# A decoder layer's second norm: rows scaled on ScalarE, the norm's weights put on in the copy of turned rows, and each block turned once

## The chip, the cores and the metric

One core of a Trainium2 chip runs the whole kernel. The metric is the device time of one execution in microseconds (us), lower is better. Five engines work side by side, each in the order of its own queue: TensorE (PE, with its weight loads PEld), VectorE (DVE), ScalarE (ACT), GpSimd (POOL) and SyncE (SP), which issues most transfers. Matmuls write to PSUM; the other tiles lie in SBUF.

## The reference, cut to what matters

One layer on 512 rows of 1024 numbers. What the change touches lies between the attention half and the MLP:

```python
def _rms_norm(x, gain):
    y = xf * lax.rsqrt(jnp.mean(xf * xf, axis=-1, keepdims=True) + NORM_EPS)
    return y * gain
# after the output projection o:
x1 = x + _rms_norm(o, attn_post_norm)
h  = _rms_norm(x1, ffn_pre_norm)          # "the second norm"
a, u = h @ ffn_w_gate, h @ ffn_w_up       # both 1024 x 4096
# then conv over three rows on a, gelu(a) * u, @ ffn_w_down, post norm, residual add
```

So each row of `h` is a row of `x1` times one scalar of that row (1/rms), times a vector of 1024 weights that is the same for all rows.

## The kernel before, in words

All matmuls are done in three passes: every operand is split into a high part (`hi`, a ScalarE copy to the matmul type) and a low part (`lo`, the VectorE difference of the operand and its high part), and hi·hi, hi·lo and lo·hi are added up.

The gate and up products use a scheme with seven products in place of eight (Strassen's kind). The rows of `h` are cut in two halves of 256 rows (half 0 is tiles t = 0, 1; half 1 is t = 2, 3) and in two halves of 512 columns (n = 0, 1). This gives four blocks 11, 21, 12, 22 (first digit the column half, second digit the row half). The right operands of the products are, turned so that columns lie on the partitions: 21, 11, t3, t1, t2, t4, 22, where with p the scaled rows t1 = p12 − p11, t3 = p22 − p12, t2 = p22 − p11 and t4 = p21 − t2. `first_products` does 21 and 11 for two pairs of weight tiles (four products of 24 matmuls), `other_products` the five others. The weights come as `pair` tiles (two transfers of 1 MB, gate and up) in a pool of five 1 MB buffers with tag `v`; `Weights.operand` splits them, hi on ScalarE (L191), lo on VectorE (L194), and GpSimd makes sums and differences of weight blocks (L177). There are four buffers for split weights, given back when a product is done.

The stage of the change: `out_rest` finishes the output projection of a tile (L405 to L407, added on VectorE at L1217). `second_norm(t)` then squares on ScalarE (L1225), takes 1/rms on GpSimd (L1231, after a small VectorE sum at L1228 or L1230), multiplies by the first norm's weights (L1241, GpSimd for t = 1 to 3), adds the residual (L1244, VectorE), squares again, takes the second 1/rms, and writes the normalised rows over `part[t][n]` in one VectorE instruction that multiplies by the scalar and by the weights of the second norm (L1247). The weights lie as rows copied to all partitions in `gains`, one `v` buffer that holds both norms' weights; two transfers of 0.5 MB fill it. `right_operand` turns two tiles of one block with eight 128x128 transposes on TensorE into two PSUM banks (L1257), copies hi from PSUM (L1259) and takes lo from PSUM and hi (L1260). It is called seven times, so there are 56 transposes. `other_operands` takes the differences between scaled rows first (L1284: six on VectorE, two on GpSimd) and turns the results.

A scheduler orders each engine's queue by priorities and by its own estimate of times; `second_norm` and `other_operands` have raised priority. `gpar`, a small tile with a norm's weights by partition, already holds the second norm's weights in its columns 8 to 15; before the change they are not read. Most tiles of 128x512 that are named here come from one pool, `F`, with 18 buffers.

Of the kernel before, what the change touches and what calls it, by code (L numbers as in the profile page):

```python
# [11 lines left out]
F32 = mybir.dt.float32  # L12
BF16 = mybir.dt.bfloat16
F32R = mybir.dt.float32r
AF = mybir.ActivationFunctionType
ALU = mybir.AluOpType
# [3 lines left out]
D = 1024  # L20
# [9 lines left out]
def f32(ap):  # L30
    return ap.bitcast(F32)
# [22 lines left out]
GV = (0,)  # L54
PLO = (1,)
MLO = 1
TS = (3,)
RAWS = 2
WARM = (18, 14, 8)
OWN = (2, 3)  # L60
# [170 lines left out]
def kernel(  # L231
# [6 lines left out]
    vec, act, pool, pe, sp = nc.vector, nc.scalar, nc.gpsimd, nc.tensor, nc.sync  # L238
# [5 lines left out]
    vpool = ctx.enter_context(tc.tile_pool(name="big", bufs=BIGS))  # L244
# [7 lines left out]
    def nm(s):  # L252
        cnt[0] += 1
        return f"{s}_{cnt[0]}"
# [3 lines left out]
    def bank(tag):  # L258
        if tag == "pv":
            turn[0] ^= 1  # L260
            tag = ("va", "vb")[turn[0]]
        return psum.tile([128, 512], F32, tag=tag, name=nm(tag), bufs=1 if tag[0] == "v" else 2)

    def tt(name, tag="F"):
        return acts.tile([128, S], F32R, tag=tag, name=nm(name), bufs={"F": FB, "M": MB, "H": HB}[tag])

    def tf(name):
        return f32(tt(name))
# [14 lines left out]
    def later(*fs):  # L283
        side.extend(fs)
        asked[0] += len(fs)
# [84 lines left out]
    ident = cst.tile([128, 128], F32, name="ident")  # L370
# [33 lines left out]
    def mm3(o, lh, ll, rh, rl, first, last):  # L404
        pe.matmul(o, lh, rh, start=first, stop=False)  # L405
        pe.matmul(o, lh, rl, start=False, stop=False)  # L406
        pe.matmul(o, ll, rh, start=False, stop=last)  # L407

    gpar = cst.tile([128, 16], F32, name="gpar")
# [5 lines left out]
    for n in range(2):  # L415
        ps = bank("sc")
        for _ in range(WARM[n]):
            keep(pe.transpose(ps[:, 0:128], ident, ident))
        if n == 0:
            ps = bank("tr")  # L420
# [35 lines left out]
    def mm_bank():  # L456
        flush(marks.popleft())
        return bank("mm")

    def mm_done():  # L460
        marks.append(asked[0])
# [133 lines left out]
    ps = bank("tr")  # L595
# [41 lines left out]
    part = [[None, None] for _ in range(4)]  # L637
# [225 lines left out]
    gains = []  # L863

    def fill_out():
        for n, a in enumerate((attn_post, ffn_pre)):
            if n == 0:
                gains.append(vpool.tile([128, 2, D], F32, tag="v", name="gains"))
            sp.dma_start(gains[0][:, n, :], a.partition_broadcast(128).rearrange("p a d -> p (a d)"))
        W.open_pairs(vpool)  # L870
        W.spare = {u: lambda: [tt("wa", "H") for _ in range(2)] for u in W.spare}
        for n in range(2):
            ws = [W.take() for _ in range(2)]
            for t in range(4):
                ps = mm_bank()
                sl = slice(128 * t, 128 * t + 128)
                for k in range(4):
                    w = ws[k // 2]
                    mm3(ps, mixT[0][k][:, sl], mixT[1][k][:, sl], w[0][:, k % 2, :], w[1][:, k % 2, :], k == 0, k == 3)
                    if t == 3 and k % 2:  # L880
                        W.free()
                    yield 1
                part[t][n] = tf("part")
                later(lambda ps=ps, t=t, n=n: act.activation(part[t][n], ps, AF.Copy))
                mm_done()
        yield "out"

    def everything():
        yield from fill_moba()
        yield from fill_nsa()  # L890
        yield from fill_diff()
        yield from fill_swa()
        yield from fill_out()
# [69 lines left out]
    class Task:  # L963
        first, mid, second, end, srcs, pv = (), None, (), None, None, None
# [222 lines left out]
    for time, _, f, rate in events:  # L1187
        owed += (time - at) * (cur if at < now else late_rate)
        at = time
        k = int(owed)  # L1190
# [11 lines left out]
    x1 = [fp.tile([128, D], F32, name=f"x1_{t}") for t in range(4)]  # L1202
    for t in range(4):
        act.dma_start(x1[t], x[0, 128 * t:128 * t + 128, :])
    t2pool = ctx.enter_context(tc.tile_pool(name="t2", bufs=XB))
    gpost, gpre = gains[0][:, 0, :], gains[0][:, 1, :]

    flush()
    ws = [W.take() for _ in range(4)]
# [24 lines left out]
    def half_of(a, n):  # L1234
        return a[:, 512 * n:512 * n + 512]

    def second_norm(t):
        r = rstd2(*part[t])
        for n in range(2):
            eng = vec if t in GV else pool  # L1240
            eng.tensor_tensor(part[t][n], part[t][n], half_of(gpost, n), op=ALU.mult)  # L1241
        for n in range(2):
            xh = half_of(x1[t], n)
            vec.scalar_tensor_tensor(xh, part[t][n], r, xh, ALU.mult, ALU.add)  # L1244
        r = rstd2(x1[t])
        for n in range(2):
            vec.scalar_tensor_tensor(part[t][n], half_of(x1[t], n), r, half_of(gpre, n), ALU.mult, ALU.mult)  # L1247

    def right_operand(src, tags, tag):

        hi, lo = [], []
        for m in range(2):
            ps = bank(tags[m])
            for k in range(2):
                for u in range(2):
                    c = 128 * (2 * m + k)
                    pe.transpose(ps[:, 256 * k + 128 * u:256 * k + 128 * u + 128], src[u][:, c:c + 128], ident)  # L1257
            h, l = (t2pool.tile([128, S], F32R, tag="X", name=nm("fT")) if tag == "X" else tt("fT", tag) for _ in range(2))
            act.activation(h, ps, AF.Copy)  # L1259
            vec.tensor_sub(l, ps, f32(h))  # L1260
            for k in range(2):
                hi.append(h[:, 256 * k:256 * k + 256])
                lo.append(l[:, 256 * k:256 * k + 256])
        return hi, lo

    R = {}
    for half in range(2):
        for n in range(2):
            for t in (2 * half, 2 * half + 1):
                out_rest(t, n)  # L1270
            if half:
                W.free(2)
        for t in (2 * half, 2 * half + 1):
            with tc.high_priority(HN):
                second_norm(t)
        if not half:
            R["11"] = right_operand([part[0][0], part[1][0]], ("tr", "pv"), "M")
            R["21"] = right_operand([part[0][1], part[1][1]], ("tr", "pv"), "M")

    def other_operands():  # L1280
        tags = ("tr", "pv")
        p = part
        def less(n, o, a, b):
            (pool if n in TS else vec).tensor_tensor(o, a, b, op=ALU.subtract)  # L1284

        t2 = [tf("t2") for _ in range(2)]
        for t in range(2):
            less(0, p[t][0], p[t + 2][0], p[t][0])
            less(1, p[t + 2][0], p[t + 2][1], p[t + 2][0])
            less(2, t2[t], p[t + 2][1], p[t][0])  # L1290
            less(3, p[t][1], p[t][1], t2[t])
        R["t3"] = right_operand([p[2][0], p[3][0]], tags, "H")
        R["t1"] = right_operand([p[0][0], p[1][0]], tags, "H")
        R["t2"] = right_operand(t2, tags, "H")
        R["t4"] = right_operand([p[0][1], p[1][1]], tags, "H")
        R["22"] = right_operand([p[2][1], p[3][1]], tags, "X")


    acc = []
# [94 lines left out]
    with tc.high_priority(HN):  # L1394
        other_operands()
# [83 lines left out]
```

## Time and profile before

| what | value |
|---|---|
| time, median of 3 runs | 822.89 us (821.38 to 822.95) |
| the profiled execution | 821.32 us, its span 819.5 us |
| instructions | 13505 |
| busy: PE, DVE, ACT, POOL | 781.0, 665.6, 446.9, 338.5 us |

The span is the time from the first to the last instruction in the trace; 1.8 us lie around it. Times within the trace are counted from the span's start. A busy PE is not PE at its peak, and idle time of an engine that nobody waits for costs nothing. The second norm lies between about 270 and 326 us.

### The profile page before, as it was taken

To read this page: it belongs to the slowest core of one execution; us is meant where nothing else is said; L and a number is where in the kernel's file an instruction comes from. 1 tells how busy PE (TensorE), PEld (TensorE's weight loads), DVE (VectorE), ACT (ScalarE), POOL (GpSimd) and SP (SyncE) were. 2 spreads that over 40 slices of the span, in tenths; PEclk is the share of its full clock that TensorE was granted. 3 is DMA by queue.
4 is the path that set the end of the run, shared out by engine and by line. 5 is a ranking of instruction groups with operands and counts; after the bars stand their busy time and mean duration, and the time that the engine had idled before them with its cause. 6 is when DMAs were issued, how large, how long until landed. Compare 5 with 4: busy or idle time off the path is not lost.

```text
span 819.5 us, 13505 instructions
## 1 busy us (share of the span) xinstructions
PE 781.0 (95%) x5087; PEld 712.1 (87%) x5087; DVE 665.6 (81%) x1131; ACT 446.9 (55%) x931; POOL 338.5 (41%) x309
## 2 busy tenths in 40 slices
PE   8999998999989769999999999999999999999995
PEld 8998986997868658988998998998998998998984
DVE  5657768877586999896797797897897987989857
ACT  6657666777676545645554453454454454445532
POOL 5245333336244757343343441461561561563103
PEclk9999999999989979999999999999999999999998
DMA  7455201416211403412114305216116026033212
GB/s 213 121 149 138 64 22 46 129 52 216 80 52 52 154 7 109 145 61 94 52 50 157 103 10 197 67 38 206 43 61 206 18 86 205 1 104 104 69 60 102
DMA packets 72920, 78.76 MB, mean 96 GB/s; under 512 B 7782, under 2 KB 58136, under 8 KB 72856
## 3 DMA queue, kind: packets, MB, share of 16 engines
q1 hardware_dynamic: 71032, 73.71, 29.3%
q10 hardware_dynamic: 1824, 4.20, 1.5%
q8 instruction: 40, 0.66, 0.3%
q14 instruction: 24, 0.20, 0.1%
HBM read 73.71 MB, written 2.10 MB: 93 GB/s over the span
## 4 chain that ended last, share of the span: by engine, by line
PE 57%; DVE 33%; issue 3%; DMA 3%; ACT 2%; POOL 1%; ACTq 0%; DVEq 0%; POOLq 0%
DVE wu L194 13%; PE mm L405 5%; PE mm L406 5%; PE mm L407 4%; DVE y L1362 3%; PE mm L1312 3%; PE mm L1314 3%; PE mm L1313 3%; PE tr L406 3%; PE tr L407 2%; PE sc L1314 2%; PE sc L1313 2%; PE sc L1312 2%; PE tr L405 2%; PE tr L973 2%
## 5 line engine op out<-in xcount | busy, mean ns | idle before, releaser
L194 DVE TENSOR_TENSOR wu<-pair,wu 128x512 fp32r<-128x512 f32 x188 | 174.6, 964 | 15.8 <-ACT wu L191 15.6
L191 ACT ACTIVATE wu<-pair 128x512 fp32r<-128x512 f32 x188 | 108.6, 622 | 76.3 <-PE sc L1314 19.8
L1314 PE MATMUL mm<-fT,wu 128*128 128x256 f32 x488 | 138.3, 283 | 0.7 <-DVE wu L194 0.7
L1312 PE MATMUL mm<-fT,wu 128*128 128x256 f32 x488 | 138.2, 283 | 0.7 <-ACT mo L1343 0.7
L1313 PE MATMUL mm<-fT,wu 128*128 128x256 f32 x488 | 138.2, 283 | 0.0
L1314 PE MATMUL sc<-fT,wu 128*128 128x256 f32 x392 | 111.3, 284 | 0.0
L1313 PE MATMUL sc<-fT,wu 128*128 128x256 f32 x392 | 111.1, 284 | 0.0
L1312 PE MATMUL sc<-fT,wu 128*128 128x256 f32 x392 | 111.0, 284 | 0.0
L152 ACT ACTIVATE wu<-raw 128x512 fp32r<-128x512 f32 (+2 forms) x126 | 71.3, 609 | 67.9 <-DMA raw<-in_ffn_w_down_dram 43.8
L177 POOL TENSOR_TENSOR sum<-pair 128x512 f32<-128x512 f32 x32 | 48.7, 1526 | 141.2 <-DMA pair<-in_ffn_w_up_dram 71.4
L177 POOL TENSOR_TENSOR pair<-sum,pair 128x512 f32<-128x512 f32 x32 | 56.2, 1771 | 116.6 <-DVE wu L194 114.7
L177 POOL TENSOR_TENSOR pair<-pair 128x512 f32<-128x512 f32 x64 | 103.4, 1628 | 2.0
L157 DVE TENSOR_TENSOR wu<-raw,wu 128x512 fp32r<-128x512 f32 (+2 forms) x96 | 73.5, 783 | 35.3 <-ACT wu L152 34.8
L1312 PEld LDWEIGHTS mm<-fT,wu 128*128 128x128 f32 x488 | 93.6, 192 | 1.2 <-ACT mo L1343 0.9
L1314 PEld LDWEIGHTS mm<-fT,wu 128*128 128x128 f32 x488 | 93.6, 192 | 0.9 <-DVE wu L194 0.9
L1313 PEld LDWEIGHTS mm<-fT,wu 128*128 128x128 f32 x488 | 93.6, 192 | 0.3
L941 POOL TENSOR_SCALAR P<-P,rc 128x128 f32<-128x128 f32 (+2 forms) x80 | 42.3, 547 | 84.3 <-DVE rc L1039 39.6
L1313 PEld LDWEIGHTS sc<-fT,wu 128*128 128x128 f32 x392 | 75.2, 192 | 0.3
L1312 PEld LDWEIGHTS sc<-fT,wu 128*128 128x128 f32 x392 | 75.2, 192 | 0.3
L1314 PEld LDWEIGHTS sc<-fT,wu 128*128 128x128 f32 x392 | 75.3, 192 | 0.0
L949 ACT ACTIVATE P<-P,mn 128x128 f32<-128x128 f32 (+2 forms) x96 | 52.1, 543 | 33.2 <-DVE mn L948 32.8
L157 POOL TENSOR_TENSOR wu<-raw,wu 128x512 fp32r<-128x512 f32 (+2 forms) x30 | 40.6, 1356 | 48.4 <-ACT wu L152 44.7
(318 smaller groups left out, 1955.8 us busy)
## 6 DMA issues: line engine op xcount, KB each, us to landing
pair<-in_ffn_w_gate_dram SPq DMA_DIRECT2D x16, 1024.0 KB, 7.7
pair<-in_ffn_w_up_dram SPq DMA_DIRECT2D x16, 1024.0 KB, 5.4
raw<-in_ffn_w_down_dram SPq DMA_DIRECT2D x32, 512.0 KB, 4.1
raw<-in_w_in_dram SPq DMA_DIRECT2D x14, 512.0 KB, 3.9
raw<-in_w_out_dram SPq DMA_DIRECT2D x8, 512.0 KB, 5.4
raw<-in_w_in_dram SPq DMA_DIRECT2D x10, 256.0 KB, 3.2
x<-in_x_dram SPq DMA_DIRECT2D x4, 512.0 KB, 4.6
x<-in_x_dram ACTq DMA_DIRECT2D x4, 512.0 KB
```

Of the source, the lines that this page charges most:

```text
L152: keep(self.nc.scalar.activation(box["h"][:, sl], box["r"][:, sl], AF.Copy))
L157: keep(eng.tensor_tensor(box["l"][:, sl], box["r"][:, sl], f32(box["h"][:, sl]), op=ALU.subtract))
L177: self.nc.gpsimd.tensor_tensor(block(g, out), block(g, a), block(g, b), op=op)
L191: self.nc.scalar.activation(box["h"][g], block(g, src), AF.Copy)
L194: self.nc.vector.tensor_sub(box["l"][g], block(g, src), f32(box["h"][g]))
L405: pe.matmul(o, lh, rh, start=first, stop=False)
L406: pe.matmul(o, lh, rl, start=False, stop=False)
L407: pe.matmul(o, ll, rh, start=False, stop=last)
L949: act.activation(pi, pi, AF.Exp, bias=mn[:, i:i + 1], scale=-1.0, accum_out=sm[:, i:i + 1])
L1312: pe.matmul(o, wh, rh, start=first, stop=False, skip_group_check=True)
L1313: pe.matmul(o, wh, rl, start=False, stop=False, skip_group_check=True)
L1314: pe.matmul(o, wl, rh, start=False, stop=last, skip_group_check=True)
```

## The change

- The second norm's last step is a ScalarE copy with the row's scalar as its scale. The weights are no longer read as rows; the second transfer into `gains` goes, and `gains` holds the first norm's weights alone.
- `turn_block` turns each of the four blocks once (32 transposes). Two ScalarE copies per PSUM bank, 256 columns each, bring the turned rows to SBUF and put on the weights, which are now one number per partition (a column of `gpar`). The results are new tiles `turned`, two per block.
- `right_operand` takes hi and lo from the turned tiles in SBUF.
- The differences are taken between turned tiles: six 128x512 subtractions on VectorE and two on GpSimd, as many as before.
- Block 21 is made ahead of block 11.

```diff
     def fill_out():
-        for n, a in enumerate((attn_post, ffn_pre)):
-            if n == 0:
-                gains.append(vpool.tile([128, 2, D], F32, tag="v", name="gains"))
-            sp.dma_start(gains[0][:, n, :], a.partition_broadcast(128).rearrange("p a d -> p (a d)"))
+        gains.append(vpool.tile([128, D], F32, tag="v", name="gains"))
+        sp.dma_start(gains[0], attn_post.partition_broadcast(128).rearrange("p a d -> p (a d)"))
...
         r = rstd2(x1[t])
         for n in range(2):
-            vec.scalar_tensor_tensor(part[t][n], half_of(x1[t], n), r, half_of(gpre, n), ALU.mult, ALU.mult)
-
-    def right_operand(src, tags, tag):
-
-        hi, lo = [], []
+            act.activation(part[t][n], half_of(x1[t], n), AF.Copy, scale=r)
+
+    turned = {}
+
+    def turn_block(half, n):
+
+        ys = turned[half, n] = [tf("turned") for _ in range(2)]
         for m in range(2):
-            ps = bank(tags[m])
+            ps = bank(("tr", "pv")[m])
             for k in range(2):
                 for u in range(2):
                     c = 128 * (2 * m + k)
-                    pe.transpose(ps[:, 256 * k + 128 * u:256 * k + 128 * u + 128], src[u][:, c:c + 128], ident)
+                    pe.transpose(ps[:, 256 * k + 128 * u:256 * k + 128 * u + 128], part[2 * half + u][n][:, c:c + 128], ident)
+            for k in range(2):
+                c, g = slice(256 * k, 256 * k + 256), 8 + 4 * n + 2 * m + k
+                act.activation(ys[m][:, c], ps[:, c], AF.Copy, scale=gpar[:, g:g + 1])
+
+    def right_operand(src, tag):
+
+        hi, lo = [], []
+        for y in src:
             h, l = (t2pool.tile([128, S], F32R, tag="X", name=nm("fT")) if tag == "X" else tt("fT", tag) for _ in range(2))
-            act.activation(h, ps, AF.Copy)
-            vec.tensor_sub(l, ps, f32(h))
+            act.activation(h, y, AF.Copy)
+            vec.tensor_sub(l, y, f32(h))
...
         if not half:
-            R["11"] = right_operand([part[0][0], part[1][0]], ("tr", "pv"), "M")
-            R["21"] = right_operand([part[0][1], part[1][1]], ("tr", "pv"), "M")
+            for n in (1, 0):
+                turn_block(0, n)
+                R["12"[n] + "1"] = right_operand(turned[0, n], "M")
 
     def other_operands():
-        tags = ("tr", "pv")
-        p = part
-        def less(n, o, a, b):
-            (pool if n in TS else vec).tensor_tensor(o, a, b, op=ALU.subtract)
-
+        def less(o, a, b, eng=vec):
+            for m in range(2):
+                eng.tensor_tensor(o[m], a[m], b[m], op=ALU.subtract)
+
+        for n in (1, 0):
+            turn_block(1, n)
+        y11, y21, y12, y22 = (turned[a, n] for a in range(2) for n in range(2))
         t2 = [tf("t2") for _ in range(2)]
-        for t in range(2):
-            less(0, p[t][0], p[t + 2][0], p[t][0])
-            less(1, p[t + 2][0], p[t + 2][1], p[t + 2][0])
-            less(2, t2[t], p[t + 2][1], p[t][0])
-            less(3, p[t][1], p[t][1], t2[t])
-        R["t3"] = right_operand([p[2][0], p[3][0]], tags, "H")
-        R["t1"] = right_operand([p[0][0], p[1][0]], tags, "H")
-        R["t2"] = right_operand(t2, tags, "H")
-        R["t4"] = right_operand([p[0][1], p[1][1]], tags, "H")
-        R["22"] = right_operand([p[2][1], p[3][1]], tags, "X")
+        less(y11, y12, y11)
+        less(y12, y22, y12)
+        R["t3"] = right_operand(y12, "H")
+        R["t1"] = right_operand(y11, "H")
+        less(t2, y22, y11)
+        R["t2"] = right_operand(t2, "H")
+        less(y21, y21, t2, pool)
+        R["t4"] = right_operand(y21, "H")
+        R["22"] = right_operand(y22, "X")
```

## Rows read from the trace of the kernel before

**Rows 1.** The page: busy time of each engine over the span, and the chain that ended last, by engine.

```profile
PE 781.0 (95%) x5087; PEld 712.1 (87%) x5087; DVE 665.6 (81%) x1131; ACT 446.9 (55%) x931; POOL 338.5 (41%) x309
PE 57%; DVE 33%; issue 3%; DMA 3%; ACT 2%; POOL 1%; ACTq 0%; DVEq 0%; POOLq 0%
```

**Rows 2.** Busy time of each engine by stretches of the stage. Columns: stretch, its length, busy time and (instructions) of PE, PEld, DVE, ACT and POOL, the granted TensorE clock as a share of full speed, DMA share, GB/s.

```profile
270.00:282.60 12.60, 12.20 (x53) 9.44 (x51) 12.57 (x17) 8.14 (x19) 11.60 (x9) 1.00 0.45 172
282.60:296.00 13.40, 2.38 (x10) 1.55 (x10) 13.40 (x20) 4.17 (x11) 8.40 (x8) 0.69 0.00 0
296.00:306.00 10.00, 9.66 (x71) 9.05 (x70) 10.00 (x15) 4.78 (x9) 4.71 (x4) 0.90 0.01 2
306.00:316.00 10.00, 8.63 (x73) 8.25 (x72) 10.00 (x13) 5.58 (x12) 7.84 (x5) 1.00 0.35 107
316.00:326.00 10.00, 9.22 (x77) 8.81 (x75) 10.00 (x14) 5.61 (x11) 7.81 (x6) 1.00 0.21 62
326.00:340.00 14.00, 13.92 (x116) 13.92 (x117) 11.79 (x18) 8.16 (x14) 2.95 (x2) 1.00 0.37 116
```

**Rows 3.** Waits from 270 to 345 us: who waited for whom, us in total, times, the longest.

```profile
PE tr L1257 <- DVE part L1247: 10.0, 2, 6.6
PE tr L1257 <- DVE part L1284: 1.4, 2, 0.8
```

**Rows 4.** The chain of waits through the stage in order of time: start, us, engine, tile and line.

```profile
288.48 2.34 DVE part L1247 x2
...
295.64 2.65 DVE x L1244 x4
...
300.80 4.80 DVE part L1247 x4
305.60 1.80 DVE part L1284 x3
...
320.31 0.66 PE vb L1257 x4
```

**Rows 5.** VectorE's groups by form from 200 to 340 us, the one that is removed: line, engine, operation, out<-in, shapes, count, busy us, mean ns, idle before.

```profile
L1247 DVE SCALAR_TENSOR_TENSOR part<-x,r,gains 128x512 f32<-128x512 f32 x8 | 8.6, 1129 | 0.0
```

**Rows 6.** VectorE's groups by form from 306 to 326 us, same columns: the weights' low parts, whose two inputs lie in SBUF, and the operands' low parts, of which one input lies in PSUM.

```profile
L194 DVE TENSOR_TENSOR wu<-pair,wu 128x512 fp32r<-128x512 f32 x8 | 9.0, 1162 | 0.0
L1260 DVE TENSOR_TENSOR fT<-tr,fT 128x512 fp32r<-128x512 f32 x5 | 3.4, 675 | 0.0
```

**Rows 7.** VectorE in order of time: start, us (of all that the row merges), line, operation.

```profile
305.53 1.88 DVE L1284 TENSOR_TENSOR part<-part,part 128x512 f32<-128x512 f32 x3
...
311.42 0.67 DVE L1260 TENSOR_TENSOR fT<-vb,fT 128x512 fp32r<-128x512 f32 x1
...
321.97 2.39 DVE L194 TENSOR_TENSOR wu<-pair,wu 128x512 fp32r<-128x512 f32 x2
324.28 0.68 DVE L1260 TENSOR_TENSOR fT<-vb,fT 128x512 fp32r<-128x512 f32 x1
```

**Rows 8.** GpSimd in order of time, same columns.

```profile
288.46 3.48 POOL L1241 TENSOR_TENSOR part<-part,gains 128x512 f32<-128x512 f32 x2 [1.76 <-ACT junk L1225]
...
294.25 1.13 POOL L1231 TENSOR_TENSOR r<-r,mhalf 128x1 f32<-128x1 f32 x2
300.22 1.72 POOL L1231 TENSOR_TENSOR r<-r,mhalf 128x1 f32<-128x1 f32 x2 [4.85 <-DVE r L1230]
```

**Rows 9.** ScalarE in order of time: two copies out of PSUM with a column of `gpar` as scale, from the kernel's start, and the second norm's squares of t = 2 and 3.

```profile
9.45 0.47 ACT L445 ACTIVATE hT<-vb,gpar 128x256 fp32r<-128x256 f32 x1
9.80 0.48 ACT L445 ACTIVATE hT<-tr,gpar 128x256 fp32r<-128x256 f32 x1
...
297.74 1.05 ACT L1225 ACTIVATE junk<-x 128x1024 bf16<-128x1024 f32 x1
...
299.26 1.06 ACT L1225 ACTIVATE junk<-x 128x1024 bf16<-128x1024 f32 x1
```

**Rows 10.** ScalarE's groups by form from 200 to 340 us: a copy of 128x512 from SBUF to SBUF, and one from PSUM.

```profile
L191 ACT ACTIVATE wu<-pair 128x512 fp32r<-128x512 f32 x20 | 11.5, 623 | 7.0 <-PE sc L1314 4.1 <-issue 2.2 <-PE mm L407 0.4
...
L1259 ACT ACTIVATE fT<-tr 128x512 fp32r<-128x512 f32 x7 | 4.2, 596 | 10.2 <-PE tr L1257 10.1
```

**Rows 11.** TensorE in order of time: the first matmuls of `first_products`, four transposes among matmuls, the first matmul of product t3, and the first of product 22.

```profile
297.90 0.52 PE L1312 MATMUL mm<-fT,wa 128*128 128x256 f32 x2
...
313.01 0.28 PE L1313 MATMUL sc<-fT,wu 128*128 128x256 f32 x1
313.13 0.60 PE L1257 MATMUL tr<-ident,t 128*128 128x128 f32 x4
313.49 0.36 PE L1314 MATMUL sc<-fT,wu 128*128 128x256 f32 x1
313.69 0.28 PE L1312 MATMUL sc<-fT,wu 128*128 128x256 f32 x1
...
314.05 0.28 PE L1312 MATMUL mm<-fT,wu 128*128 128x256 f32 x1
...
330.49 0.28 PE L1312 MATMUL sc<-fT,wu 128*128 128x256 f32 x1
```

**Rows 12.** SyncE's waits from 200 to 420 us, the one for the buffer of `gains`.

```profile
SPq L104 <- DVE part L1247: 39.7, 1, 39.7
```

**Rows 13.** GpSimd in order of time: its wait for a transfer of weights.

```profile
328.06 1.66 POOL L177 TENSOR_TENSOR sum<-pair 128x512 f32<-128x512 f32 x1 [4.25 <-DMA pair<-in_ffn_w_up_dram]
```

More of the change, by code (lines that the diff above doesn't have):

```diff
@@ L56 @@
 MLO = 1
-TS = (3,)
 RAWS = 2
@@ L1205 @@
     t2pool = ctx.enter_context(tc.tile_pool(name="t2", bufs=XB))
-    gpost, gpre = gains[0][:, 0, :], gains[0][:, 1, :]
+    gpost = gains[0]
     flush()
```

## The prediction

> **What bounds the kernel now.** I read the page first: TensorE is busy for 95% of the span, yet of the chain that ended last 33% is VectorE [rows 1]. So there are stretches in which TensorE waits, and the table by stages is to find them. From 282.6 to 296 us TensorE works 2.38 of 13.4 us, and from 306 to 326 it misses 1.37 and 0.78 us, while VectorE has no idle time from 282.6 to 326; only from 326 on is it the other way round, TensorE at 13.92 of 14, VectorE at 11.79 [rows 2]. The waits say for whom TensorE stands still: 10.0 us for L1247, the very instruction that the change moves, and 1.4 us for the differences of L1284 [rows 3]. The chain in order of time runs through VectorE from the first L1247 at 288.48 on and goes over to TensorE with the transposes at 320.31 [rows 4]. A gain has to be made before that point; what the chain lacks there is not VectorE's time as such but the order of steps that ends in the turned operands.
>
> **Removed.** Eight L1247, 8.6 us of VectorE, 1.13 us each [rows 5]. Of the transposes 24 of 56. Four of them start at 313.13, the next matmul comes at 313.49, and its successor 0.20 us later, where matmuls follow each other every 0.12 us elsewhere (313.01 to 313.13): 0.36 + 0.08 = 0.44 us for four [rows 11], so 24 cost 2.6 us of TensorE.
>
> **Added on ScalarE.** Eight scalings of 128x512 from SBUF to SBUF, 0.62 us each as L191 [rows 10]: 5.0 us. Sixteen copies of 256 columns out of PSUM with a column of `gpar` as scale; the kernel's start has this very form, 0.47 us, one every 0.35 us in a row [rows 9]: 5.6 us. The fourteen hi copies read SBUF in place of PSUM, 0.62 for 0.60 [rows 10]: 0.4 us. Together 11 us, in a stage in which ScalarE works 4.17 of 13.4 and 4.78 of 10 us [rows 2]. They cost nothing as work; they cost where a row waits in ScalarE's queue.
>
> **The fourteen lo subtractions.** Their count and size stay, but both inputs now lie in SBUF. Out of PSUM they take 0.675 us while GpSimd is busy beside them for 7.84 and 7.81 of 10 us; the weights' lo, the same shape with both inputs in SBUF, takes 1.162 us in the same stretch [rows 2, 6]. So each can cost between 0 and 0.49 us more. Ten of them fall behind 306 us: 0 to 4.9 us. I take half, 2.4, because as VectorE takes longer the last of them come after GpSimd's run, which does not grow.
>
> The Trainium skill, page "SBUF — State Buffer", section "Who interferes with whom", says that a VectorE instruction with two SBUF inputs and a GpSimd instruction that reads SBUF shut each other out for the whole instruction, while one with at most one SBUF input never contends. The trace agrees on both sides (0.675 against 1.162 us). By the page every one of the ten would be exposed, and the sum would be the first rival's, no gain; by half the price it is the forecast.
>
> **Where the second half's rows come.** VectorE's 2.34 us at 288.48 fall away, but what follows waits on GpSimd: two multiplications from 288.46, then the scalars, the last ending at 294.25 + 1.13 = 295.38, so the residual additions start at 295.4 where they start at 295.56 now [rows 4, 8]. Then come ScalarE's squares (297.74 and 299.26) and the scalars from 300.22, the last at 301.94 [rows 8, 9]. Now L1247 writes the four tiles until 300.80 + 4.80 = 305.60 [rows 4]. On ScalarE the last two scalings need 1.24 us: 303.2 at the earliest. At the latest the first half's eight turned copies (2.8 us) stand ahead of all this: 306.0. I take 304.2, nearer to the early end since ScalarE has half of this stretch free.
>
> **Operand t3.** Now it is ready at 311.42 + 0.67 = 312.1 [rows 7], and its product starts at 314.05 [rows 11], so it is TensorE's own queue that is late: the first products ran from 297.90 to 314.05 with twenty transposes in between and the 1.4 us of waits. After the change sixteen transposes stand there: 0.44 and 1.4 us less, and 0.2 from the earlier start, 2.0 us. For the operand: 304.2, transposes 0.44, six copies 2.1 (the first subtraction needs block 22 and half of block 12), 306.7; four subtractions at 0.6, hi 0.62, lo 0.67: 310.4 unheld, and with the six VectorE instructions held half of the time (6 × 0.24) 311.9. It fits under TensorE's 312.05. So t3 starts 2.0 us earlier.
>
> **The products after t3.** TensorE has no transposes there any more, five groups of four, another 2.2 us: its limit is 4.2 us. VectorE's limit: now it works from the first difference at 305.53 to the last lo for product 22 at 324.96, 19.4 us, and the weights for it are split at 324.36 [rows 7]; product 22 starts at 330.49 [rows 11]. After: 306.7 + 19.4 + 2.4, less 0.6 for one addition of products (L1333) that finds room before, is 327.9, so product 22 can start 2.6 us earlier; with the ends of the lo's price 325.5 (5.0 earlier) and 330.4 (0.1). I take 2.6 as the smaller of the two limits, and give back 0.4 for the clock: it is granted at 0.69 and 0.90 around the first products, so partly at the lower of its levels of 1.2 and 2.4 GHz, after TensorE had stood still [rows 2, 3]; the transposes now come with gaps for the copies, and the rise may come later (0 to 1 us). Sum: −2.2 us.
>
> **At no cost.** The second transfer into `gains` goes. It also frees that buffer after L1241 in place of L1247; SyncE waited 39.7 us for L1247 to issue a weight transfer [rows 12], which can now start some 11 us earlier. But the wait of GpSimd that follows, 4.25 us until 328.06, is for the other transfer of that pair [rows 13], and TensorE runs through it, so nothing is gained. If the cover were gone, the most it could cost is these 4.25 us. The eight turned tiles, eight scaled ones and two of t2 fill the 18 buffers exactly; the next user takes a tile of the first half, long turned. GpSimd's two subtractions come after t2, now as before, and its weight sums queue behind them; nobody needs those before about 330 us.
>
> **How this stands to the runs.** The sum is made against the profiled 821.32 us (span 819.5 and 1.8 around it): 819.1. That execution lay 1.57 us under the median, so for the median 822.89 − 2.2 = 820.7 us. A difference within 0.2%, 1.65 us, can hardly be told from none.
>
> **Rivals.**
> First: GpSimd holds off every lo (1.162 each). VectorE ends at 330.4, product 22 starts where it did: 822.8, same. For it: GpSimd is busy 78% of the stretch. Against: half of these subtractions may move to its pauses.
> Second, slower: ScalarE becomes the chain. Rows scaled at 306.0, and lo's held: 306.0 + 0.44 + 2.1 + 19.4 + 4.9 − 0.6 = 332.2 against 330.5, +1.7 us or, if the second half's copies too queue behind weight splits (0.62 us each, two per product), about +3: 825.0 at the middle. It decides from rows scaled after 304.3 with full holds, or after 306.8 with half. For it: squares, scalings, copies and hi's of both halves meet from 295 to 308. Against: ScalarE's free time.
> Third, TensorE's limit is reached: lo's hardly held, −4.2 us: 818.7. For it: VectorE loses 8.6 us of work.
> Fourth: the 2.2 us are made and given back behind 326 us, where VectorE still works 84% [rows 2] and the weights' splits pace it: 822.9, same. Against: TensorE has no gaps there [rows 2].
>
> **Chances.** Forecast 0.43 (819.3 to 821.3), first 0.17, second 0.18, third 0.12, fourth 0.10. Faster: 0.43 less 0.04 for its edge, 0.12 of the third: 0.51. Slower: 0.18 and the first's upper edge, 0.01: 0.19. Same: 0.30. The range reaches from just under the third to the middle of the second: 818.2 to 825.0.
>
> **What would show it.** L1247 gone from VectorE and VectorE idle for several us between 288 and 306; scaled rows at 303 to 306; lo's above 0.68 us in the mean; t3's product some 2 us earlier relative to the stage's start, and no transposes after it. The prediction is wrong if the scheduler orders ScalarE or GpSimd otherwise than I assume around 286 to 300, above all if the first half's rows or the squares wait behind new copies.

## The result, and the profile after

The changed kernel takes 830.47 us in the median (830.03 to 832.21, 4 runs), 7.6 us more than before; the ratio to before is 1.0101, its 95% interval 1.0082 to 1.0119. The profiled execution took 830.69 us with a span of 828.9. In the text of the kernel after, L1244 is the scaling on ScalarE (was L1247 on VectorE), L1256 the transposes, L1259 the turned copies, L1266 and L1267 the hi and lo parts, L1291 the differences, L193 the weights' low parts, L1321 to L1323 the product matmuls.

The page, first line and first line of the chain:

```profile
PE 780.5 (94%) x5063; PEld 711.3 (86%) x5063; DVE 664.7 (80%) x1123; ACT 458.0 (55%) x955; POOL 339.0 (41%) x309
PE 63%; DVE 27%; issue 3%; ACT 3%; DMA 2%; POOL 1%; ACTq 0%; DVEq 0%; POOLq 0%; SPq 0%
```

ScalarE has 11.1 us more than in [rows 1], just what was worked out. VectorE, which lost the 8.6 us of L1247, has only 0.9 us less: something that stayed on it became dearer by nearly 8 us.

The stretches of the stage, columns as in [rows 2]:

```profile
270.00:282.60 12.60, 12.15 (x53) 9.40 (x51) 12.57 (x16) 8.16 (x19) 11.66 (x9) 1.00 0.45 172
282.60:296.00 13.40, 4.20 (x16) 3.10 (x16) 11.72 (x18) 8.23 (x18) 8.49 (x8) 0.59 0.00 1
296.00:306.00 10.00, 7.01 (x48) 6.90 (x48) 4.37 (x7) 8.09 (x17) 4.18 (x5) 0.70 0.34 107
306.00:316.00 10.00, 8.16 (x68) 7.85 (x66) 6.85 (x10) 8.19 (x17) 2.25 (x2) 1.00 0.00 0
316.00:326.00 10.00, 3.04 (x12) 2.30 (x13) 10.00 (x8) 3.86 (x7) 9.31 (x7) 0.65 0.01 2
326.00:340.00 14.00, 13.31 (x99) 13.11 (x99) 13.07 (x16) 5.10 (x9) 6.29 (x4) 0.88 0.40 128
```

VectorE is idle for some 9 us between 296 and 316, where it had no idle time before, and has none from 316 to 326; TensorE works 3.04 of the 10 us after 316, where it had 9.22 [rows 2]. The loss lies there. TensorE in order of time shows it matmul by matmul:

```profile
298.99 0.58 PE L1321 MATMUL mm<-fT,wa 128*128 128x256 f32 x1 [5.41 <-ACT fT L1266]
...
309.46 0.27 PE L1256 MATMUL tr<-ident,part 128*128 128x128 f32 x1
...
310.97 0.27 PE L1256 MATMUL va<-ident,part 128*128 128x128 f32 x1
...
313.78 0.38 PE L1321 MATMUL mm<-fT,wu 128*128 128x256 f32 x1
317.61 0.38 PE L1322 MATMUL mm<-fT,wu 128*128 128x256 f32 x1 [3.44 <-DVE fT L1267]
...
321.69 0.58 PE L1321 MATMUL mm<-fT,wu 128*128 128x256 f32 x1 [3.23 <-ACT fT L1266]
...
324.92 0.58 PE L1322 MATMUL mm<-fT,wu 128*128 128x256 f32 x1 [2.13 <-DVE fT L1267]
325.30 0.42 PE L1323 MATMUL mm<-fT,wu 128*128 128x256 f32 x1
325.52 0.41 PE L1321 MATMUL mm<-fT,wu 128*128 128x256 f32 x1
...
339.87 0.28 PE L1321 MATMUL sc<-fT,wu 128*128 128x256 f32 x1
```

Product t3 begins at 313.78, no later than before (314.05 [rows 11]), but its operand isn't there: lo, then the second half's hi, then its lo are waited for, 3.44 + 3.23 + 2.13 = 8.8 us. After the standstill the matmuls follow every 0.21 us until 329 in place of 0.12 (the clock's lower level), 1.9 us for 20 of them. From t3's first matmul to product 22's first it is 26.09 us, before 16.44 [rows 11]: +9.65, and the start was 0.27 earlier, so product 22 starts 9.38 us later. The spans differ by 9.4: in the two profiled executions all of the loss is made between these two matmuls. The waits and the lower clock, less the 2.2 us of the twenty transposes that are gone from there, make 8.8 + 1.9 − 2.2 = 8.5 of the 9.65; most of the rest lies right around the standstills, where matmuls come 0.38 or 0.52 us after one another.

What t3's operand waited for, ScalarE in order of time (the first two lines are a square of the second norm, L1222, and the first turned copies of the first half):

```profile
294.36 1.06 ACT L1222 ACTIVATE junk<-x 128x1024 bf16<-128x1024 f32 x1 [1.67 <-DVE x L1241]
...
295.41 0.82 ACT L1259 ACTIVATE turned<-tr,gpar 128x256 f32<-128x256 f32 x2
...
302.99 1.34 ACT L1244 ACTIVATE part<-x,r 128x512 f32<-128x512 f32 x2 [0.76 <-POOL r L1228]
...
306.22 0.84 ACT L1259 ACTIVATE turned<-tr,gpar 128x256 f32<-128x256 f32 x2 [1.37 <-PE tr L1256]
...
310.23 0.84 ACT L1259 ACTIVATE turned<-tr,gpar 128x256 f32<-128x256 f32 x2 [0.46 <-PE tr L1256]
310.96 1.15 ACT L190 ACTIVATE wu<-pair 128x512 fp32r<-128x512 f32 x2
312.00 0.84 ACT L1259 ACTIVATE turned<-va,gpar 128x256 f32<-128x256 f32 x2
...
321.01 1.67 ACT L1266 ACTIVATE fT<-turned 128x512 fp32r<-128x512 f32 x3 [5.47 <-DVE turned L1291]
```

VectorE in the same stretch:

```profile
311.11 0.69 DVE L1291 TENSOR_TENSOR turned<-turned,turned 128x512 f32<-128x512 f32 x1 [0.61 <-ACT turned L1259]
...
314.12 1.76 DVE L1291 TENSOR_TENSOR turned<-turned,turned 128x512 f32<-128x512 f32 x1
315.81 1.75 DVE L1267 TENSOR_TENSOR fT<-turned,fT 128x512 fp32r<-128x512 f32 x1
...
319.17 1.75 DVE L1291 TENSOR_TENSOR turned<-turned,turned 128x512 f32<-128x512 f32 x1
...
323.12 5.12 DVE L1267 TENSOR_TENSOR fT<-turned,fT 128x512 fp32r<-128x512 f32 x3
```

And GpSimd:

```profile
313.75 1.59 POOL L1291 TENSOR_TENSOR turned<-turned,t 128x512 f32<-128x512 f32 x1 [9.44 <-ACT fT L1266]
315.30 3.40 POOL L176 TENSOR_TENSOR sum<-pair 128x512 f32<-128x512 f32 x2
318.66 3.39 POOL L176 TENSOR_TENSOR pair<-pair 128x512 f32<-128x512 f32 x2
...
327.65 3.43 POOL L176 TENSOR_TENSOR pair<-pair 128x512 f32<-128x512 f32 x2
```

The rows are scaled at 302.99 + 1.34 = 304.33. Their transposes run among matmuls, the turned copies wait for them and end at 312.84, t3's second difference starts at 319.17, 6.3 us after the last copy, and its last lo ends at about 324.8. From 314 to 331 VectorE's differences and lo's take about 1.75 us each, while GpSimd, which stood 9.44 us before its first subtraction, makes the weight sums that had queued behind it; two weight splits in this stretch, with two SBUF inputs as well, took 1.17 and 0.68 us, the second while GpSimd stood still.

### The profile page after: what moved, and what is told of

It is laid out like the page before. It is cut to its first block, busy times and chain, and to the rows that moved or that the text cites. A ratio compares the mean times of both kernels' runs of the same rounds, so it can differ in the third digit from the quotient of the medians.

```text
span 828.9 us, 13474 instructions
## 1 busy us (share of the span) xinstructions
PE 780.5 (94%) x5063; PEld 711.3 (86%) x5063; DVE 664.7 (80%) x1123; ACT 458.0 (55%) x955; POOL 339.0 (41%) x309
## 4 chain that ended last, share of the span: by engine, by line
PE 63%; DVE 27%; issue 3%; ACT 3%; DMA 2%; POOL 1%; ACTq 0%; DVEq 0%; POOLq 0%; SPq 0%
DVE wu L193 10%; PE mm L404 5%; PE mm L405 5%; PE mm L406 4%; PE mm L1321 4%; PE mm L1322 4%; PE mm L1323 3%; PE tr L405 3%; PE sc L1321 3%; PE sc L1322 3%; PE sc L1323 3%; PE tr L406 3%; DVE y L1371 3%; PE tr L404 3%; PE tr L970 2%
## 5 line engine op out<-in xcount | busy, mean ns | idle before, releaser
L193 DVE TENSOR_TENSOR wu<-pair,wu 128x512 fp32r<-128x512 f32 x188 | 172.0, 949 | 16.4 <-ACT wu L190 16.0
L1321 PE MATMUL mm<-fT,wu 128*128 128x256 f32 x488 | 139.2, 285 | 3.9 <-ACT fT L1266 3.2
L1323 PE MATMUL mm<-fT,wu 128*128 128x256 f32 x488 | 139.1, 285 | 0.7 <-DVE wu L193 0.7
L1321 PE MATMUL sc<-fT,wu 128*128 128x256 f32 x392 | 111.7, 285 | 0.0
L1323 PE MATMUL sc<-fT,wu 128*128 128x256 f32 x392 | 111.6, 285 | 0.0
L1321 PEld LDWEIGHTS mm<-fT,wu 128*128 128x128 f32 x488 | 94.4, 193 | 4.7 <-ACT fT L1266 3.4
L1323 PEld LDWEIGHTS mm<-fT,wu 128*128 128x128 f32 x488 | 94.5, 194 | 1.2 <-DVE wu L193 1.1
L1321 PEld LDWEIGHTS sc<-fT,wu 128*128 128x128 f32 x392 | 75.7, 193 | 0.6 <-ACT fT L1266 0.2
L1323 PEld LDWEIGHTS sc<-fT,wu 128*128 128x128 f32 x392 | 75.6, 193 | 0.0
```

The lines of the kernel that those rows point to most:

```text
L193: self.nc.vector.tensor_sub(box["l"][g], block(g, src), f32(box["h"][g]))
L1321: pe.matmul(o, wh, rh, start=first, stop=False, skip_group_check=True)
L1323: pe.matmul(o, wl, rh, start=False, stop=last, skip_group_check=True)
```

## The experiments

Four theories were set against each other. A: GpSimd's late subtractions and sums meet VectorE and make it slow. B: ScalarE's queue brings the rows or copies late. C: VectorE's order is wrong. D: turning each block once makes t3's path longer, through the queues of three engines. The expectations below were written under these names. The ratios are to the kernel before in the same series of runs, whose median lay between 820.82 and 822.85 us, so times of two series are compared by their ratios.

**The two halves of the change alone.** The first keeps before's structure and only moves the scalar: ScalarE multiplies the rows, VectorE puts the weights on.

```diff
-vec.scalar_tensor_tensor(part[t][n], half_of(x1[t], n), r, half_of(gpre, n), ALU.mult, ALU.mult)
+act.activation(part[t][n], half_of(x1[t], n), AF.Copy, scale=r)
+vec.tensor_tensor(part[t][n], part[t][n], half_of(gpre, n), op=ALU.mult)
```

> One part of the change alone: the kernel before (822.9 us), in which the rows are multiplied by their scalar on ScalarE and then by the weights on VectorE (a product of two tiles); 56 transposes, differences of rows and low parts out of PSUM as before. Theory D (the loss is in turning once: the operand of product t3 passes through two more queues, and its low parts meet GpSimd): 822 to 825. Theory B (rows late in ScalarE's queue): 826 to 829.

823.04 us, ratio 1.0016 (1.0001 to 1.0031, 10 runs). The second keeps L1247 on VectorE as before, with the weights as rows and their transfer, and turns each block once, with a plain copy of 512 columns.

```diff
-act.activation(part[t][n], half_of(x1[t], n), AF.Copy, scale=r)
+vec.scalar_tensor_tensor(part[t][n], half_of(x1[t], n), r, half_of(gpre, n), ALU.mult, ALU.mult)
-    act.activation(ys[m][:, c], ps[:, c], AF.Copy, scale=gpar[:, g:g + 1])
+act.activation(ys[m], ps, AF.Copy)
```

> The other part alone: L1247 on VectorE with scalar and weights as before, but each block turned once, copied to SBUF by ScalarE in one instruction of 512 columns without a scale, differences of turned blocks. D: 828 to 833, no better than the whole change. B: 822 to 825.

836.30 us, ratio 1.0177 (1.0148 to 1.0205). Two of TensorE's waits from 282 to 345 us in this kernel (who for whom, us in total, times, longest):

```profile
PE mm L1322 <- DVE fT L1267: 9.8, 2, 6.9
PE mm L1321 <- ACT fT L1266: 4.0, 2, 2.1
```

So turning once carries the whole loss and more; the scalar's move costs 0.2%, and beside the turning the rest of the change even helps (830.5 against 836.3), though this pair also differs in the form of the copies.

**GpSimd.** First t4's two subtractions on VectorE:

```diff
-less(y21, y21, t2, pool)
+less(y21, y21, t2)
```

> The changed kernel (830.5 us) with the two subtractions for t4 on VectorE in place of GpSimd, nothing else. Theory A (GpSimd's weight sums, held back behind those two subtractions, collide with VectorE's two-SBUF-input instructions from 314 to 331 us): the sums start at about 304 in place of 315 us and end about 10 us earlier, and the time falls to 825 to 827 us. Theory B (ScalarE's queue makes the rows and the turned copies late): 830 to 831.5, VectorE only has 1.2 us more to do. Theory C (the order on VectorE, where t2's differences and weight splits stand ahead of t3's second half): 829 to 831.

831.03 us, ratio 1.0112 (1.0089 to 1.0135): GpSimd makes its sums without the 9.44 us of standing still, and VectorE's subtractions from 318 to 330 take 0.68 us, yet nothing is won. Then the second weight pair's sums and differences left out (products of that pair get wrong weights):

```diff
 def combine(g, out, a, b, op):
+    if late:
+        if out == "s":
+            q["s", g] = block(g, "21")
+        return
```

> The changed kernel without GpSimd's sums and differences of the weights of the second pair (eight instructions from 300 to 331 us), so that pair's products are not the right ones; the rest of the work is the same. A: VectorE's instructions of this stage fall from 1.7 to 0.68 us each, t3's second half is ready about 6 us earlier, time 823 to 825.5. B: 829.5 to 830.5. C: 828 to 830.

827.93 us, ratio 1.0070 (1.0050 to 1.0090). Its control, the same edit to the kernel before:

> The kernel before with the second pair's weight sums left out: the control. If the meeting with GpSimd is a price of the change alone, before gains little, under 1 us: 821 to 822. If before paid the same price, it gains the same 2.6 us: 819, and the meeting explains nothing of the difference.

820.03 us, ratio 0.9976 (0.9964 to 0.9988). Before gains 1.7 us by it, after 2.5: without any of these sums the change still costs 0.9% (1.0070 / 0.9976). By these medians the meeting with GpSimd's sums explains about 1 us of the loss.

**ScalarE.** The scaling back to VectorE as a multiplication by the scalar alone:

```diff
-act.activation(part[t][n], half_of(x1[t], n), AF.Copy, scale=r)
+vec.tensor_scalar(part[t][n], half_of(x1[t], n), r, None, ALU.mult)
```

> The changed kernel with the scaling of the rows moved back to VectorE (one instruction with the scalar, no weights). A: 829 to 831, since the stretch from 314 to 331 stays as it is. B: ScalarE loses 5 us of work between 287 and 304, block 21's first high part comes at 296 in place of 298.3 and the first products start 2 to 3 us earlier, time 826 to 828. C: 829 to 831.

832.50 us, ratio 1.0134 (1.0101 to 1.0167). All turned copies on VectorE:

```diff
-act.activation(ys[m][:, c], ps[:, c], AF.Copy, scale=gpar[:, g:g + 1])
+vec.tensor_scalar(ys[m][:, c], ps[:, c], gpar[:, g:g + 1], None, ALU.mult)
```

> The changed kernel with the sixteen copies of turned rows on VectorE, which stands idle for some 10 us between 288 and 312. B and D as far as ScalarE's queue makes the operands late: block 21's first high part comes at 295.5 in place of 298.3, block 12 at 309 to 310 in place of 312.8, time 825 to 828. If the chain is as long on VectorE, and the collision with GpSimd (2.5 us of the loss by the run without weight sums) is all that counts: 830 to 831.

829.72 us, ratio 1.0097 (1.0074 to 1.0120), and with t4's subtractions on VectorE too:

> The same with the two subtractions for t4 on VectorE as well, so that GpSimd's weight sums run from about 303 us on. If both causes add up: 823 to 826, at best that of the kernel before. If the lateness alone counts: as the run before it, within 1 us.

831.21 us, ratio 1.0109 (1.0079 to 1.0139). The first products start 2 us earlier with the copies on VectorE, and t3's product then waits 4.58 + 1.77 us. B falls: taking 5.6 us off ScalarE is worth 0.7 us by the medians and 0.3 by the ratios (1.0101 and 1.0097), which is within the noise.

**The order and length of t3's chain.** VectorE's differences and these lo's kept in the order of the text:

```diff
-eng.tensor_tensor(o[m], a[m], b[m], op=ALU.subtract)
+keep(eng.tensor_tensor(o[m], a[m], b[m], op=ALU.subtract))
-vec.tensor_sub(l, y, f32(h))
+keep(vec.tensor_sub(l, y, f32(h)))
```

> The changed kernel with VectorE's differences and low parts kept in the order of the program, so that t2's differences come after t3's and t1's low parts. A: the instructions stay at 1.7 us each, 829 to 832. B: 830 to 831. C: t3's second difference comes 3 to 5 us earlier, time 825.5 to 828.

831.59 us, ratio 1.0121 (1.0096 to 1.0146). Then t3 in tiles of its own, ahead of t1, with the order kept as in the run before:

```diff
-less(y11, y12, y11)
-less(y12, y22, y12)
-R["t3"] = right_operand(y12, "H")
+t3 = [tf("t3") for _ in range(2)]
+less(t3, y22, y12)
+R["t3"] = right_operand(t3, "H")
+less(y11, y12, y11)
```

> t3 is written to tiles of its own, so its two differences no longer wait for those of t1, and stand ahead of them on VectorE; the rest as after. Theory D, in the form that the chain of differences makes t3 late: block 12's copies end at about 312.8, two differences and the two lo's at 0.7 to 1.75 us each give 315.5 to 319, so TensorE's waits in the t3 product fall from 8.8 us to 3 to 6, and the time is 825 to 828. Theory A, in the form that the meeting with GpSimd sets the price whatever the order: each of these still takes 1.75 us and what is saved at the front comes back at t1's operand: 829 to 831.

830.13 us, ratio 1.0094 (1.0063 to 1.0125). With half of the turned copies on VectorE as well:

> The short t3 chain, and half of the turned copies on VectorE, which is idle for about 10 us in that stretch. Block 12's two last copies no longer stand behind one another: some 0.6 to 1.2 us earlier than in the kernel with the short chain alone, 824 to 827 by theory D; if the transposes' place in TensorE's queue sets the copies, no difference from that kernel.

830.23 us, ratio 1.0103 (1.0071 to 1.0134). And t3's operand made from block 12 with no difference (so this product is another one):

```diff
-less(y11, y12, y11)
-less(y12, y22, y12)
 R["t3"] = right_operand(y12, "H")
+less(y11, y12, y11)
```

> The t3 operand is made from block 12 itself, with no difference (the output is another one); all other differences stay. If the differences on turned blocks are what is late: t3's hi and lo follow the copies at 312.8, so at 314 to 315 they are ready, TensorE waits 0 to 2 us there, and the time is 821.5 to 825 (the meeting with GpSimd is left for t1). If the transposes and copies that stand behind other work are as large a part, or the wait only moves to t1's operand: 827 or more.

831.02 us, ratio 1.0113 (1.0078 to 1.0149). TensorE's waits in that kernel:

```profile
PE mm L1320 <- ACT fT L1266: 5.4, 1, 5.4
PE mm L1321 <- DVE fT L1267: 3.7, 2, 2.4
PE sc L1321 <- DVE fT L1267: 2.1, 1, 2.1
```

The 5.4 us are those before the first products. The wait for t3's second difference is gone, but its lo's are still waited for (3.7 us), and now also t1's (`sc`, 2.1). So the differences alone don't make t3 late: what follows is late as well. The orders also had a flaw that the trace shows: in the kernel with the short chain t3's differences stood on VectorE behind the addition that ends the second first product, whose copy on ScalarE ran at 313.90.

**The clock.** After, with 2 times 24 transposes that nobody reads among the matmuls of t3:

```diff
 less(y12, y22, y12)
+ps = bank("tr")
+for m in range(2):
+    for _ in range(24):
+        pe.transpose(ps[:, 0:128], y12[m][:, 0:128], ident)
```

> After, with 2 times 24 transposes into a spare bank that nobody reads, put between the matmuls of t3's product, so that TensorE has work while it waits for t3's operand. If the lower clock after the wait is part of the price: the 20 matmuls from 324.9 to 329.2 go at 0.12 us apart in place of 0.21, and the time falls by up to 1.9 us, to about 828.6. If the clock is no part of it (what follows waits for something else anyway): 830.5, or above by what the transposes delay.

831.96 us, ratio 1.0124 (1.0092 to 1.0156). The clock was 1.00 from 326 to 340 in place of 0.88, but the second group itself took 4.28 us, from 322.45 on, longer than the standstill of 2.13 or 3.23 us that it was to fill. This decides nothing: what the clock gave, the transposes may have taken.

**Several at once.** Short chain and no weight sums:

> The short t3 chain of the earlier run and the second pair's weight sums left out, together. If t3's late chain and the meeting with GpSimd cover each other (each alone gives little: 830.1 and 827.9 us were measured), the two together give more than their sum: 824 to 826. If the price lies ahead of both (block 12's transposes and copies, which end at about 312.8): no more than the weight sums alone, 827 to 828.

827.38 us (824.06 to 828.50), ratio 1.0065 (1.0042 to 1.0087): no more than the sums alone in the median. Short chain, and the second half's transposes kept ahead of the second first product:

```diff
-firsts = [first_products(tag) for tag in ("mm", "sc")]
+firsts = [first_products("mm")]
+for n in (1, 0):
+    turn_block(1, n, keep)              # keep: in the order of the text on TensorE
+firsts.append(first_products("sc", keep))
```

> The short t3 chain, and the second half's 16 transposes ahead of the second first-product group (48 matmuls) on TensorE, so they run as soon as the rows are there (304.3) and no copy waits for a transpose behind matmuls. If the transposes' place sets it: block 12's copies end at 308.5 to 309.5 in place of 312.8, t3 is ready at 312 to 314, and the time falls by 2 to 4 us, to 826 to 828.5. If VectorE's work from there on sets it: 829.5 to 831.

833.14 us, ratio 1.0140 (1.0119 to 1.0160); the transposes still ran only from 309.95 on, behind 48 matmuls, which ran at the lower clock until 306.3 (0.21 us apart). The same with t4's subtractions on VectorE:

> The one before, with t4's two subtractions on VectorE, so that GpSimd makes its weight sums from 302 on, while VectorE mostly waits. Two causes that add up: 2 to 3 us below the kernel with the transposes first, 824 to 826. If VectorE's amount of work sets it, the two subtractions more cost 1.4 us: 828 to 831.

828.15 us, ratio 1.0081 (1.0058 to 1.0105). Last, the transposes behind 24 matmuls only, and t3's differences and lo's ahead of the additions that end the first products:

```diff
 product(bb, "21", True, keep)
+if between:                              # in the first of the two: turn_block(1, n, keep)
+    between()
 product(ba, "11", True, keep)
...
 R["t3"] = right_operand(t3, "H")
+for end in ends:                         # the copy and addition of each first product
+    end()
```

> The second half's 16 transposes stand behind the first 24 matmuls only, t3's two differences and lo's stand on VectorE ahead of the additions that end the first products, t4's subtractions are on VectorE. If t3's chain (queues that it stands in) is the cause: transposes at 304.5, copies 305.5 to 309, t3 ready at about 312.5 to 313.5, before TensorE has done the 72 matmuls left (about 315), so the waits inside t3's product go from 8.8 us to under 1.5, and the time is 820 to 823.5. If something else makes turned blocks dear (VectorE's amount of work, ScalarE's): 826 or more.

827.57 us, ratio 1.0077 (1.0058 to 1.0096). With GpSimd's subtractions where the change has them:

> As f5 with t4's subtractions on GpSimd as in the change, so its weight sums run from about 311 on beside VectorE's operations with two SBUF inputs. If the meeting is dear when t3 is on time: 2 to 4 us above f5, in waits for lo's of t1 and t2. If it is covered then: within 1 us of f5.

833.50 us, ratio 1.0144 (1.0121 to 1.0166). VectorE in the kernel with the chain freed, and below it in the one with GpSimd's subtractions:

```profile
311.69 1.49 DVE L1267 TENSOR_TENSOR fT<-turned,fT 128x512 fp32r<-128x512 f32 x1 [0.22 <-ACT fT L1266]
315.68 1.29 DVE L193 TENSOR_TENSOR wu<-pair,wu 128x512 fp32r<-128x512 f32 x2 [2.50 <-ACT wu L190]
316.89 1.29 DVE L1291 TENSOR_TENSOR t<-turned,turned 128x512 f32<-128x512 f32 x2
...
328.30 1.29 DVE L1267 TENSOR_TENSOR fT<-t,fT 128x512 fp32r<-128x512 f32 x2
```

```profile
328.12 3.53 DVE L193 TENSOR_TENSOR wu<-pair,wu 128x512 fp32r<-128x512 f32 x2 [1.10 <-ACT wu L190]
331.58 3.44 DVE L1267 TENSOR_TENSOR fT<-t,fT 128x512 fp32r<-128x512 f32 x2
```

TensorE in the kernel with the chain freed:

```profile
298.87 0.58 PE L1322 MATMUL mm<-fT,wa 128*128 128x256 f32 x1 [5.41 <-ACT fT L1266]
...
308.62 0.60 PE L1256 MATMUL va<-ident,part 128*128 128x128 f32 x4
...
321.79 0.42 PE L1322 MATMUL mm<-fT,wu 128*128 128x256 f32 x1 [3.94 <-DVE c L1347]
```

Here GpSimd is worth 5.9 us (833.50 against 827.57), and 5.0 us in the pair before it (833.14 against 828.15), while in the change's own order it was worth nothing (831.03 against 830.47): its price differs from order to order, and why is not shown. By its expectation, 826 us or more with the chain freed would speak for another cause than t3's queues. That can't be concluded here, as t3 wasn't freed: the last copy ended at 311.1, but t3's differences began only at 316.89, now behind a weight split that waited for a split buffer, which TensorE gives back when a product ends. TensorE had its first products done at about 317.85 in place of 314.05, as they ran in part at the lower clock (0.50 from 296 to 306) with their operands awaited, and then stood 3.94 us for the addition that frees a PSUM bank. 3.8 + 3.9, less 2.2 for the 20 transposes gone from behind t3's start, is 5.5 us; its span is 5.6 us over that of before.

What is shown: turning the blocks once costs all of the loss, it costs it in every one of the orders and splits that were run (827.4 to 833.5 us, all above before), and the two engines first blamed, GpSimd and ScalarE, explain it in no run by themselves. In the trace of the change the loss is t3's operand, late on a path through three engines. What stays open: which part of that path weighs most, and whether some order hides it, as no run took the path away. In each run where one wait was taken away, another stood behind it.

## Why the prediction was wrong, step by step

**Right.** ScalarE's 11 us (11.1 on the page), which cost little as work (the kernel with the scalings alone: 823.04; the change without the turned copies on ScalarE: 829.72). VectorE's idle time ahead of the second half. The gains' transfer and the buffer moved nothing: the whole difference of the spans is made before product 22. The rows of the second half at 304.2 (304.33), partly by luck: ScalarE's queue made the last square late, as thought (300.01 in place of 299.26), but a weight sum on GpSimd also stood ahead of the last scalar, which came at 302.96 in place of 301.94, and that was not counted.

**Half right: TensorE's 2.0 us ahead of t3.** The first products with the sixteen transposes among them took 313.78 − 298.99 = 14.8 us where they had taken 16.15 with twenty [rows 11]: 1.36 us less, where 1.84 were forecast. But they began 1.09 us later, not 0.2 earlier: TensorE waited 5.41 us for ScalarE, whose copies of the first half, transposed by 293.6, began at 295.41, behind a square that itself waited for VectorE. So t3's product began 0.27 us earlier, not 2.0.

**The step that failed: operand t3, ready at 311.9.** It was ready at about 324.8. Two terms of it were wrong.

The first is "transposes 0.44, six copies 2.1, 306.7". The sixth copy ended at 311.07, 4.4 us later, and the eighth at 312.84. I put the transposes at the moment their rows were there, and gave no price to their place in TensorE's queue, in which they stand among the first products' matmuls: those of block 12 came from 309.46 to 311.2. In the kernel before the same queue delayed transposes too, but there the differences were already made, on VectorE, which didn't have to wait for TensorE in between. After the change the path goes TensorE, ScalarE, VectorE, ScalarE, VectorE, and stands behind other work on each.

The second is "four subtractions at 0.6, hi 0.62, lo 0.67, held half of the time (6 × 0.24)". VectorE took from 311.11 to 324.8 for it, 13.7 us where 5.2 were forecast, which is 8.5 us more and with the 4.4 makes the 12.9 us by which t3 was late: weight splits, an addition of products and t2's difference stood in between, and each held instruction took 1.75 us. My upper bound for being held, 0.49 us, was the mean of eight weight splits [rows 6], some held and some free. A mean over both is no upper end. A single one in the trace of before had it:

```profile
290.81 1.69 DVE L194 TENSOR_TENSOR wu<-sum,wu 128x512 fp32r<-128x512 f32 x1
```

VectorE's groups by form from 282 to 340 us, after, show the lo's at 1.05 and 1.77 us in the mean, where out of PSUM they took 0.675 [rows 6]:

```profile
L1267 DVE TENSOR_TENSOR fT<-turned,fT 128x512 fp32r<-128x512 f32 x12 | 12.2, 1052 | 6.5 <-ACT fT L1266 6.5
L1267 DVE TENSOR_TENSOR fT<-t,fT 128x512 fp32r<-128x512 f32 x2 | 3.5, 1770 | 0.0
```

That is 6.3 us more for the fourteen, nearly all of it in the ten behind 306 us, for which I took 2.4 and allowed 4.9. I took half because I thought that GpSimd's run would end before VectorE's last lo's. It began later instead, behind t2: its last weight sums of that run ended at 327.65 + 3.43 = 331.08, in the kernel before at 323.81:

```profile
319.06 4.75 POOL L177 TENSOR_TENSOR pair<-pair 128x512 f32<-128x512 f32 x3
```

The Trainium skill, page "SBUF — State Buffer", section "Who interferes with whom", says that the lock is held for the whole instruction; the trace agrees, as 1.75 us is the instruction's 0.68 plus 1.07, most of the 1.30 us that one of GpSimd's takes alone. The prediction's "never contends" is wider than that section, which excepts VectorE's 2-port modes and gives a subtraction of two tensors none.

**"At no cost": GpSimd's two subtractions come after t2, now as before.** They did, but t2 itself came later (it is p22 − t1, not p22 − p11 as stated at the start, so it stands behind t1's difference too). GpSimd stood 9.44 us where it had stood 3.1, and its sums, for which nobody waited, then ran against most differences and lo's. In this kernel taking its subtractions away gave nothing; in the two orders with the transposes ahead it gave 5 to 6 us.

**The clock.** 0.4 us was given back for it, for the first products. After the standstill in t3's product 20 matmuls ran at the lower level, 1.9 us; that follows from the step that failed.

**The rivals.** The slower case came, but not by its mechanism: the rows were there at 304.3, for which with full holds its own sum gives no loss, and 5.6 us less work on ScalarE gave at most 0.7 us back. Only a small part of it was there: block 12's last two copies, transposed at 311.2, began at 312.00, behind two weight splits. The first rival (each lo held) came true for six of the ten lo's behind 306 us, at 1.7 us each, and would have given no change; the loss came from the path in front of them, which no rival had.

## What to carry to other kernels

When a step that an engine did early is put behind a transpose and a copy, count the queues on the new path and price the wait in each of them, from the moment that the input is there to the moment that the last reader has its tile; the sum of work of each engine says little. Take the upper end of a contention's price from single instructions, never from a group's mean. And split a change into its halves first: two runs told more here than all that took a single cause away, since with several waits in a row a removed wait can uncover the next.

## What the runs showed of the hardware

A VectorE 128x512 subtraction with two SBUF inputs took 0.68 us beside an idle GpSimd and about 1.75 us beside GpSimd's instructions in a row; GpSimd's took 1.70 us each there and 1.30 alone. Small instructions pay it too: in the trace of the change the 128x1 addition of a row's two sums took 0.16 us at 289.61, just ahead of a GpSimd multiplication, and 1.22 us at 294.25, in the middle of one. Matmuls of 256 columns follow every 0.12 us at the clock's upper level and every 0.21 at the lower.
